# Seven block products in place of eight in the turned projections of a two-layer encoder step

## The chip, the cores and the metric

The kernel runs on one core of one Trainium2 chip. The metric is device microseconds of one execution, the median of the runs. Engines are named as the profile does: PE is TensorE (matrix products and transposes), DVE is VectorE, ACT is ScalarE, POOL is GpSimd, SP is SyncE, which issues most DMAs; each runs its own queue in order.

## What is computed

A step of an encoder with two layers, over 2048 prompt tokens and 64 new frames ("sample"), d = 1024, 16 heads of 64, in float32.

```python
q, k, v, gate = split(rms_norm(x, norm_a) @ w_in_a, 4)      # layer a, 1024 -> 4 x 1024
o = band_attend(q, k, v, rel_bias_a)                          # own chunk of 64 and 8 before it
x = x + (o * silu(gate)) @ w_out_a
k, v = split(rms_norm(x, norm_kv) @ w_kv, 2)                  # shared keys and values of layer b
q, gate = split(rms_norm(x, norm_b) @ w_in_b, 2)
o = stick_breaking_attend(q, [cache_b_k, k], [cache_b_v, v])
y = rms_norm(x + (o * silu(gate)) @ w_out_b, norm_f)
```

Outputs are y for prompt and sample, and the new keys and values of both layers. The inputs are drawn at random in float32, as are the weights.

## The kernel before

The program is one instruction stream per engine. Four stages follow one another: projections of layer a, its attention (with the output projection and the late jobs beside it), projections of layer b, its attention.

**Numbers in two parts.** A float32 operand of a product is held as h + l in the format fp32r: ScalarE copies x to h, VectorE makes l = x - h (`split`, line 211; with the norm's weight as a factor, `scaled_split`). A product of two such operands is three matmuls per block of 128 inputs, hh, hl and lh (`mm3`, line 229), 24 for 1024 inputs.

**Projections** (`projections`, line 240) run twice, for `L` "a" and "b". The tokens are two halves of 1024 (`HALF`); the 64 new frames stand behind the first half's columns. First come the *values*: for each of 17 tiles of 128 tokens x is loaded, normed (`normed`), transposed on TensorE (`turned`) and split (`parted`) into `x_own` (first half) or `x_big` (second half); with x as the stationary operand and 512 columns of value weights moving, 24 matmuls give 512 value columns of a tile. All 17 tiles pass for the first 512 columns, then again for the second. In layer a the values are split and stored; in layer b they are written out and into a scratch tensor `v_raw`.

Then come the *turned* projections, whose results stand with features on partitions and tokens along the row (keys, queries, gates). A job is one kind and one head pair (`hp`, 128 output columns), 24 jobs per layer. Its weights are loaded raw by ScalarE's DMA queue, scaled and split to `wh`, `wl`, and are stationary; x moves. The first half with the new frames takes chunks of 364, 362 and 362 columns, the second half two of 512 (`HALVES`). Each chunk has a PSUM bank of its own (`ps_t`, tag `mm`, five banks), which ScalarE and VectorE split (gates: SiLU) into a row buffer that is stored. Some jobs of the second half are not made here (`DEFER`): keys in a, gates and queries in b. They are the *late jobs* that run beside the attention (`late_job`, line 736; `lwh`, `lwl`, `ps_j`), in a with raw weights loaded again into `lraw` (buffer tag `og`), in b with split weights that the first stage stored (`KEPT`). Keys are also turned back into rows by TensorE for the output (`natural`, `ps_n`, `kn`).

**Staged work** is spread between the jobs by count (`stages`): caches are loaded, transposed or differenced, split and stored for the attention (`stage_cache`, `stage_bias`, `stage_diff`, `stage_w_out`). Layer b's attention uses differences of neighbouring value rows. For the cached rows, `stage_diff` ("cache") loads two shifted tiles and subtracts on GpSimd; for the new ones ("new", 34 steps) it does the same from `v_raw`, in layer b's turned stage.

**Order.** Inside the attention stages the order of every engine's instructions is written out by hand (`order`, `Beat`). In the projections the compiler's scheduler orders them by its own estimate of times, starting from the program's order. Buffers with the same tag share memory in a ring of `bufs`; a new tile waits for the last use of the one it replaces. `opool` holds the tags `oh`, `ol`, `og`, `xr`, `big` holds two tiles of 32 KB per partition that are x of the second half, later the output weights.

## Time and profile before

| what | us |
|---|---|
| median of 3 runs | 3265.88 (3264.77 to 3266.47) |
| the profiled execution, its time | 3270.1 |
| its span, first to last instruction | 3268.3 |
| values of a | 9.3 to 212.5 |
| turned projections of a | 212.5 to 678.7 |
| attention of a | 678.7 to 1418.6 |
| values of b | 1418.6 to 1621.2 |
| turned projections of b | 1621.2 to 2019.8 |
| attention of b | 2019.8 to 3268.3 |

How to read it: in a row of a group, the number behind x is the count, then come busy time in us, the mean ns of one instruction, and idle time of the engine before them with what ended it. A row of a window has its bounds and length, the busy time and count of PE, PEld (weight loads), DVE, ACT and POOL, the granted TensorE clock (1.00 is full speed), the share of the DMA engines and GB/s; a window asked for one tile counts that tile's instructions alone. A row of the timeline has start, duration, engine, line, operation, out<-in, shape and count. Matmuls are pipelined: a 512-column one shows some 0.39 us, while the next starts well before its end, so the cost of one in a stream is the distance between starts. Nearly all lines are L92, the helper through which the engines are called, so groups are told apart by their tiles.

### The profile page before, as it was taken

What the parts mean: (1) busy time and instruction counts of PE and PEld (TensorE: products, weight loads), DVE (VectorE), ACT (ScalarE), POOL (GpSimd) and SP (SyncE); (2) the same over time, 40 slices, a digit from 0 to 9 for tenths busy, and PEclk for the clock granted to TensorE, in tenths of its full rate; (3) what the DMA queues carried; (4) which work ended last, traced back from release to release, by engine and by line L of the source; (5) the groups of instructions that cost most, each with busy time, mean ns of one, the idle gap of its engine ahead of it and who ended that gap; (6) DMA issues with size and microseconds to landing.
All of it is one profiled execution on the core that took longest, in us unless ns stands there. A gap on an engine that the chain in (4) does not pass through costs nothing.

```text
span 3268.3 us, 53340 instructions
## 1 busy us (share of the span) xinstructions
PE 3199.2 (98%) x17928; PEld 2784.4 (85%) x17928; DVE 1872.0 (57%) x3786; ACT 1711.0 (52%) x3719; POOL 1291.8 (40%) x1950
## 2 busy tenths in 40 slices
PE   8999999999998999999999999999999999999999
PEld 7889999988887898878889999788888888888877
DVE  4225431157777776232043333788878888888873
ACT  5234322258887776143143442566666666666662
POOL 3001210035655554020044200344467777777761
PEclk9999999999999999999999999999999999999999
DMA  6359972387899993554399998977835566355523
GB/s 203 121 184 362 345 280 79 118 248 218 237 259 263 245 237 117 173 178 133 109 342 358 347 349 291 247 211 197 217 121 158 147 193 194 117 144 143 136 72 120
DMA packets 457209, 671.08 MB, mean 205 GB/s; under 512 B 48885, under 2 KB 258837, under 8 KB 456934
## 3 DMA queue, kind: packets, MB, share of 16 engines
q1 hardware_dynamic: 395174, 608.14, 60.9%
q10 hardware_dynamic: 61760, 59.52, 5.6%
q8 instruction: 143, 2.34, 0.3%
q14 instruction: 132, 1.08, 0.1%
HBM read 408.78 MB, written 258.76 MB: 204 GB/s over the span
## 4 chain that ended last, share of the span: by engine, by line
PE 76%; issue 7%; DVE 6%; DMA 6%; ACT 2%; POOL 2%; SPq 0%; POOLq 0%; ACTq 0%; DVEq 0%
PE ps_t L92 24%; PE ps_v L92 11%; PE acc L92 10%; PE z L92 9%; PE wt L92 9%; PE ps_j L92 6%; PE ps_o L92 5%; DVE s L92 2%; DVE pl L92 2%; DMA kt<-k_b 1%; PE ps_tr L92 1%; DMA q<-q_a 1%; DMA keys<-k_a 1%; DMA gate_b<-sg 1%; ACT ph L92 1%
## 5 line engine op out<-in xcount | busy, mean ns | idle before, releaser
L92 DVE TENSOR_TENSOR pl<-wt,ph 128x512 fp32r<-128x512 f32 (+1 forms) x864 | 552.0, 655 | 110.9 <-ACT ph L92 107.2
L92 ACT ACTIVATE ph<-wt 128x512 fp32r<-128x512 f32 (+1 forms) x864 | 485.2, 578 | 194.9 <-PE wt L92 180.7
L92 PE MATMUL ps_t<-x_own,wh 128*128 128x362 f32 (+1 forms) x2304 | 568.4, 327 | 0.0
L92 PE MATMUL wt<-ident,s 128*128 128x128 f32 x3472 | 552.2, 274 | 10.3 <-DVE pl L92 6.7
L92 PEld LDWEIGHTS wt<-ident,s 128*128 128x128 f32 x3472 | 418.2, 141 | 86.4 <-DVE pl L92 13.6
L92 ACT ACTIVATE f<-z 128x512 f32<-128x512 f32 (+4 forms) x680 | 355.0, 535 | 199.5 <-PE z L92 134.2
L92 PEld LDWEIGHTS ps_t<-x_own,wh 128*128 128x128 f32 x2304 | 405.0, 188 | 1.8
L92 POOL TENSOR_TENSOR s<-f,s 128x256 f32<-128x256 f32 x416 | 360.5, 868 | 102.5 <-DVE s L92 93.8
L92 PE MATMUL z<-kt,q 128*128 128x512 f32 (+3 forms) x1280 | 373.1, 379 | 9.8 <-DMA q<-q_b 5.3
L92 PE MATMUL acc<-ph,vt 128*128 128x512 f32 (+3 forms) x1088 | 374.5, 379 | 4.6 <-ACT ot L92 2.4
L92 PE MATMUL ps_t<-x_own,wl 128*128 128x362 f32 (+1 forms) x1152 | 376.6, 327 | 0.0
L92 PE MATMUL acc<-pl,vt 128*128 128x512 f32 (+3 forms) x1088 | 363.7, 367 | 9.2 <-DVE pl L92 9.0
L92 POOL TENSOR_SCALAR s<-s,rc 128x640 f32<-128x640 f32 (+5 forms) x264 | 201.5, 768 | 429.5 <-DMA q<-q_a 223.5
L92 PE MATMUL ps_o<-big,oh 128*128 128x512 f32 x1088 | 336.2, 392 | 0.0
L92 POOL TENSOR_TENSOR two<-f 128x256 f32<-128x256 f32 x416 | 259.4, 625 | 164.0 <-ACT f L92 149.3
L92 DVE TENSOR_TENSOR_SCAN s<-two,s,own 128x256 f32<-128x256 f32 x408 | 300.3, 739 | 36.7 <-POOL two L92 35.4
L92 PEld LDWEIGHTS z<-kt,q 128*128 128x128 f32 x1280 | 220.6, 190 | 40.7 <-ACT f L92 11.1
L92 PE MATMUL ps_j<-big,lwh 128*128 128x512 f32 x768 | 245.7, 396 | 1.2 <-DVE pl L92 0.6
L92 PE MATMUL ps_t<-big,wh 128*128 128x512 f32 x768 | 238.9, 391 | 0.0
L92 PEld LDWEIGHTS ps_o<-big,oh 128*128 128x128 f32 x1088 | 202.4, 188 | 41.0 <-DVE pl L92 0.2
L92 PEld LDWEIGHTS acc<-pl,vt 128*128 128x128 f32 x1088 | 194.3, 190 | 41.9 <-DVE pl L92 25.7
L92 DVE CUSTOM_DVE_ANT_0 s<-z,bias 128x640 f32<-128x640 f32 (+4 forms) x256 | 184.8, 733 | 73.9 <-PE wt L92 53.3
(148 smaller groups left out, 5510.3 us busy)
## 6 DMA issues: line engine op xcount, KB each, us to landing
vt<-v_b SPq DMA_DIRECT2D x80, 512.0 KB, 5.2
v_b<-vs SPq DMA_DIRECT2D x64, 512.0 KB, 6.4
q<-q_a SPq DMA_DIRECT2D x128, 256.0 KB, 5.9
q<-q_b SPq DMA_DIRECT2D x128, 256.0 KB, 4.3
vt<-v_a SPq DMA_DIRECT2D x48, 512.0 KB, 7.9
kt<-k_b SPq DMA_DIRECT2D x96, 256.0 KB, 5.7
keys<-k_a SPq DMA_DIRECT2D x80, 256.0 KB, 7.4
v_a<-vs ACTq DMA_DIRECT2D x32, 512.0 KB, 2.7
```

What stands on the lines that cost most here:

```text
L92: ins = op(*args, **kwargs)
```

## The change

It rearranges `projections` and what feeds it.

1. **Seven products for eight.** Two head pairs (256 output columns) and the two chunks of 512 tokens of one half, over two halves of the 1024 inputs, are a 2 x 2 by 2 x 2 block product. Strassen's scheme (in Winograd's form) makes it with seven block products. Each is 4 input blocks x 3 matmuls of 512 columns. Sums of x (`mix`: adds on GpSimd and VectorE, then splits) are made during the values, differences of weights (`weights_of`) per pair on GpSimd; results are put together in PSUM (bank `x` is added to three times, bank `z` twice) and on VectorE.
2. **One half at a time.** Values of the first half and the new frames, then 12 pairs; values of the second half, then 8 pairs (a) or 4 (b). The value weights are loaded and split in each half. Raw weights come for a pair, 2 x 512 KB; they are scaled on GpSimd before the split.
3. **The new frames** are no longer columns of a moving operand: `x_new` (h and l side by side) is stationary and 256 weight columns move, 16 matmuls per pair of the first half, then two transposes.
4. **Differences of the new values** are made with the values: a DMA inside SBUF shifts the tile by one row, one row goes through `v_raw`, VectorE subtracts, and the split result is stored from SyncE's queue. `stage_diff` keeps the cached rows only.
5. **Staged work** is spread anew: a's first half takes caches, biases and eight key caches, a's second half 16 differences of the cache, b's first half the other 16 and the other key caches, b's second half the output weights. `big1` becomes three tiles (`Pieces`). `x_own` loses the new frames' columns. Stored weights (b) have the pair's layout.

```diff
+            def mix(hf, u, tmp):
...
+                for x, k0, c in zip(tmp, (0, 0, 4, 4), (c1, c2, c2, c1)):
+                    h, l = xs[hf]
+                    for ks, part in rows_of(l, k0, slice(c, c + P)):
+                        whole = f32(h[:, k0 + ks.start : k0 + ks.stop, c : c + P])
+                        gps.tensor_tensor(x[:, ks], whole, f32(part), ALU.add)
+                a11, a21, a22, a12 = tmp
+                dve.tensor_tensor(a22, a21, a22, ALU.add)
+                split(*into(hf, 0, u), a22)
+                dve.tensor_tensor(a21, a11, a21, ALU.subtract)
+                if hf:
+                    split(*into(hf, 3, u), a21)
+                dve.tensor_tensor(a11, a22, a11, ALU.subtract)
+                split(*into(hf, 1, u), a11)
+                dve.tensor_tensor(a12, a12, a11, ALU.subtract)
+                split(*into(hf, 2, u), a12)
...
+                prev = vps[i % 2]
+                nc.sync.dma_start(prev[1:n], vn[: n - 1])
+                nc.sync.dma_start(vraw[r0 + n : r0 + n + 1, cols], vn[n - 1 : n])
...
+                else:
+                    nc.sync.dma_start(prev[0:1], vraw[r0 : r0 + 1, cols])
+                dve.tensor_tensor(prev[:n], prev[:n], vn, ALU.subtract)
+                store(prev[:n], nc.sync.dma_start)
...
+                def scale():
+                    for k in range(NK):
+                        r = raw[k // 4][:, k % 4]
+                        gps.tensor_scalar(r, r, g[:, k : k + 1], 1.0, ALU.mult, ALU.mult)
+
+                def whole(i):
+                    split(*forms[i], raw[i].rearrange("p k (b c) -> p b k c", b=2))
...
+                def less(i, out, x, y):
+                    gps.tensor_tensor(out, x, y, ALU.subtract)
+                    split(ts[i][:, 0], ts[i][:, 1], out)
+
+                return load, scale, [
+                    partial(whole, 0),
+                    partial(less, 0, r1[:, :, up], r1[:, :, up], r1[:, :, lo]),
+                    partial(whole, 1),
+                    partial(less, 1, r2[:, :, up], r2[:, :, up], r1[:, :, up]),
+                    partial(less, 3, r2[:, :, lo], r2[:, :, lo], r2[:, :, up]),
+                    partial(less, 2, r1[:, :, lo], r2[:, :, up], r1[:, :, lo]),
+                ]
+
+            def times(ps, x, w, begin):
+                for k in range(4):
+                    mm(ps, w[0](k), x[0](k), start=(begin and k == 0), stop=False, skip_group_check=True)
+                    mm(ps, w[0](k), x[1](k), start=False, stop=False, skip_group_check=True)
+                    mm(ps, w[1](k), x[0](k), start=False, stop=(k == 3), skip_group_check=True)
...
+                def plain(ps):
+                    c = pool.tile([P, CH], F32, name="c", tag="c", bufs=CS[L])
+                    act.activation(c, ps, AF.Copy)
+                    return c
+
+                def leave(b, t0, src):
+                    at = slice(r0 + t0 * CH, r0 + t0 * CH + CH)
+                    hl = pool.tile([P, 2, CH], F32R, name="hl", tag="hl", bufs=4)
...
+                    split(hl[:, 0], hl[:, 1], src)
+                    put(L, kind, hp + b, at, hl)
+                    row = hf * HALF + t0 * CH - first
+                    if kind == "k" and row >= 0:
+                        natural(pool, src, 0, P, 4, prompt[row : row + CH, (hp + b) * P : (hp + b) * P + P])
...
+                x = psum.tile([P, CH], F32, name="ps_x", tag="mm", bufs=5)
+                times(x, quarter(hf, 0, 0), w11, True)
+                c1 = plain(x)
+                between(0)
+                nn = new_frames() if hf == 0 else None
+                z = psum.tile([P, CH], F32, name="ps_z", tag="mm", bufs=5)
+                times(z, mixed(hf, 0), t1, True)
+                c5 = plain(z)
+                between(1)
+                times(x, mixed(hf, 1), t2, False)
+                u2 = plain(x)
+                if hf == 0:
+                    new_turned(nn)
+                between(2)
+                times(z, mixed(hf, 2), w22, False)
+                dve.tensor_tensor(u2, z, u2, ALU.add)
+                leave(1, 0, u2)
+                between(3)
+                times(x, mixed(hf, 3), t3, False)
+                dve.tensor_tensor(c5, x, c5, ALU.add)
+                leave(1, 1, c5)
+                between(4)
+                y = psum.tile([P, CH], F32, name="ps_y", tag="mm", bufs=5)
+                times(y, quarter(hf, 1, 0), w21, True)
+                dve.tensor_tensor(c1, y, c1, ALU.add)
+                leave(0, 0, c1)
+                between(5)
+                times(x, quarter(hf, 1, 1), t4, False)
...
+                    at = {1: 1, 2: 1, 5: 2, 6: 2}
+
+                    def between(p):
+                        if p == 0 and i + 2 < len(made):
+                            made[i + 2][0]()
+                        if p == 4 and i + 2 < len(made):
+                            made[i + 2][1]()
+                        for _ in range(at.get(p, 0)):
+                            if steps:
+                                steps.pop(0)()
+                        for _ in range(-(-len(mine) // (7 - p))):
+                            mine.pop(0)(staging["pool"])
...
+                t4 = opool.tile([P, 2, 4, P], F32R, name="t4", tag="og", bufs=1)
...
+                for i, t in enumerate(seq):
+                    if i + 2 < len(seq):
+                        parted(seq[i + 2], turned(seq[i + 2], xts(seq[i + 2])))
+                    if i >= 4 and i < 8:
+                        mix(0, i - 4, [tmp[0], tmp[4 + i - 4], tmp[1], tmp[2]])
+                    values(0, 0, i, t, vws, pool, vps)
```

`times` is one of the seven products; `quarter` and `mixed` give a block of x or a sum of blocks, `forms` the weights whole (`b1`, `b2`, made by `whole`) and their differences (`t1` to `t4`, made by `less`); `between` places the next pair's weight steps and the staged work behind product p. The last pair of the first half also loads, norms and turns the first two tiles of the second half and its value weights.

More of the change, by code (lines that the diff above doesn't have):

```diff
@@ L56 @@
 TOK = [(t * P, min(P, T - t * P)) for t in range((T + P - 1) // P)]
+VN = dict(a=2, b=4)
+XT = dict(a=4, b=3)
+CS = dict(a=5, b=4)
 HALF = NP // 2
@@ L158, in big_pair, with big_parts @@
     def big_pair():
-        return [big.tile([P, NK, D], F32R, name=f"big{i}", tag=f"big{i}") for i in range(2)]
+        return [big.tile([P, NK, D], F32R, name="big0", tag="big0"), Pieces(big_parts(F32R))]
+    def big_parts(dtype, some=(0, 1, 2)):
+        return [big.tile([P, (4, 2, 2)[i], D], dtype, name=f"bigl{i}", tag=f"bigl{i}") for i in some]
     ident = cpool.tile([P, P], F32, name="ident")
@@ L184, in encoder_step @@
             o=[dram.tile([HP, P, CH if g < GROUPS else NS], F32, name=f"o_{L}{g}") for g in range(GROUPS + 1)],
-            w={x: dram.tile([2, P, NK, P], F32R, name=f"w_{L}{x[0]}{x[1]}") for x in DEFER[L] if L in KEPT},
+            w={
+                x: dram.tile([2, 2, P, 2, 4, P], F32R, name=f"w_{L}{x[0]}{x[1]}")
+                for x in DEFER[L] if L in KEPT and x[1] % 2 == 0
+            },
         )
@@ L454, in stage_cache, with stage_diff @@
         )
-    def stage_diff(where, t, half, pool):
+    def stage_diff(t, half, pool):
         cols, heads = slice(half * CH, half * CH + CH), slice(half * 8, half * 8 + 8)
@@ L747, in load @@
                 for i, part in enumerate((st["wh"], st["wl"])):
-                    sp.dma_start(f32(part), f32(lay[L]["w"][kind, hp][i]))
+                    src = lay[L]["w"][kind, hp & ~1][i, :, :, hp & 1]
+                    sp.dma_start(
+                        f32(part).rearrange("p (h k) c -> p h (k c)", h=2), f32(src).rearrange("h p k c -> p h (k c)")
+                    )
         def cut(k0):
@@ L1058, in first_stage @@
         load_g("b", a["norm_b"][0])
-        none = pool.tile([P, CH], F32, name="vcur", tag="vr", bufs=2)
-        gps.memset(none, 0.0)
-        for c in range(0, D, CH):
-            nc.sync.dma_start(vraw[0:1, c : c + CH], none[0:1])
         stage_cache("a", 0, 0, pool)
@@ L1088, in encoder_step @@
         o["a_k_s"],
-        staged,
+        [staged, diffs[:16]],
     )
@@ L1265, in encoder_step @@
         o["b_k_s"],
-        staged_b,
+        [staged_b, outs_b],
     )
```

535 lines of the change are left out of this document (342 added, 193 removed).

## The prediction, made before the changed kernel was run

> **What bounds the kernel now.** I read the page's busy shares and slices, then the stages as windows, then single stretches of the timeline.
>
> ```profile
> span 3268.3 us, 53340 instructions
> PE 3199.2 (98%) x17928; PEld 2784.4 (85%) x17928; DVE 1872.0 (57%) x3786; ACT 1711.0 (52%) x3719; POOL 1291.8 (40%) x1950
> ```
> ```profile
> core 0: us, PE busy (x) PEld busy (x) DVE busy (x) ACT busy (x) POOL busy (x), PEclk, DMA share, GB/s
> 212.50:678.70 466.20, 465.13 (x2569) 433.92 (x2568) 144.91 (x390) 143.68 (x371) 45.80 (x43) 1.00 0.68 236
> 1418.60:1621.20 202.60, 202.06 (x928) 162.99 (x929) 38.03 (x73) 64.88 (x121) 28.57 (x34) 1.00 0.41 138
> 1621.20:2019.80 398.60, 398.18 (x2346) 379.76 (x2346) 152.78 (x321) 156.96 (x388) 90.57 (x74) 1.00 0.95 336
> ```
> The second and fourth rows are the turned projections of layers a and b. TensorE is busy for 465 of 466 us and 398 of 399; the other engines have over half of their time free. So here time is TensorE's queue, and each microsecond of matmul taken out counts, as long as nothing makes TensorE wait.
>
> **What is removed.** One job (8 input blocks, three products each) is 72 matmuls of 362 or 364 columns in the first half and 48 of 512 in the second. Two undisturbed jobs:
> ```profile
> 335.10:346.79 11.69, 11.69 (x73) 11.69 (x72) 1.75 (x3) 1.53 (x3) 1.00 0.94 327
> 346.79:357.69 10.90, 10.90 (x50) 9.02 (x49) 1.23 (x2) 1.07 (x2) 1.00 0.90 315
> ```
> So a pair of jobs takes 2 x 11.69 = 23.38 us in the first half, 21.80 in the second, and a 512-column matmul 10.90/48 = 0.227. A pair is now seven products of 12 matmuls: 84 x 0.227 = 19.07 us. In the first half come 16 matmuls of 256 columns for the new frames and two short transposes. No row has back-to-back matmuls of 256 columns in one stream; the neighbours are 128 and 320:
> ```profile
> 14.59 1.09 PE L92 MATMUL ps_tr<-ident,xt 128*128 128x128 f32 x8
> 15.44 0.48 PE L92 MATMUL ps_v<-vwl,x_own 128*128 128x512 f32 x1
> ...
> 688.27 1.33 PE L92 MATMUL z<-keys,q 128*128 128x320 f32 x8
> 689.44 0.62 PE L92 MATMUL ps_j<-big,lwh 128*128 128x512 f32 x2
> ```
> From start to next start: 0.85/8 = 0.106 and 1.17/8 = 0.146. I take 0.13, so 2.1 us (1.7 to 2.3), and 0.2 for the transposes. First half: 23.38 - 21.37 = 2.0 us a pair, 24 pairs, 48 us; the sixteen key jobs lose a sample transpose each, 16 x 0.11 = 2. Second half: 21.80 - 19.07 = 2.73, 12 pairs (8 in a, 4 in b; the rest stays in the attention), 33 us. **Gross gain 82 us** (77 to 92). Values, x transposes, cache transposes and attention keep their matmuls.
>
> **What is added beside it.** Durations:
> ```profile
> L92 POOL TENSOR_TENSOR vprev<-vprev,vcur 128x512 f32<-128x512 f32 x64 | 83.6, 1308 | 193.3 <-DMA vprev<-in_cache_b_v 133.8 <-DMA vprev<-v_raw 28.4 <-DMA vcur<-in_cache_b_v 12.3
> L92 POOL TENSOR_SCALAR s<-s,rc 128x256 f32<-128x256 f32 x16 | 7.8, 485 | 13.9 <-DVE rc L92 7.0 <-PE wt L92 4.1 <-PE z L92 2.6
> L92 ACT ACTIVATE junk<-xt 128x1024 bf16<-128x1024 f32 x32 | 33.8, 1057 | 63.6 <-DMA xt<-in_x_prompt 30.2 <-DMA xt<-x 29.7 <-issue 2.3
> L92 ACT ACTIVATE vn<-ps_v 128x512 f32<-128x512 f32 x40 | 23.7, 593 | 101.1 <-PE ps_v L92 95.9 <-DVE vs L92 4.5 <-DVE x_own L92 0.6
> L92 DVE TENSOR_TENSOR vs<-ps_v,vs 128x512 fp32r<-128x512 f32 x32 | 22.1, 691 | 99.1 <-ACT vs L92 99.1
> ```
> Per pair: GpSimd 8 scalings x 0.485 + 4 differences x 1.31 = 9.1 us. ScalarE two whole splits x 1.06, four of differences, three plain copies and four results at 0.6: 8.7, and 3.0 more for b's key rows. VectorE 4 x 0.69 + 2 x 1.38 for the splits, 3 x 0.69 sums, 4 x 0.69 results, 0.4 for the new frames: 10.8. Staged work adds 2 to 3 us to each. All of it fits into 19 to 21 us, beside TensorE; at nothing, while it comes on time.
>
> The new wait is on the accumulators. Before, each result had a bank of five to itself. Now bank x is added to again after ScalarE's copy, and only one other product, 12 x 0.227 = 2.72 us, lies between (z likewise). The copy takes 0.6, so it may start some 2 us late; then TensorE stops. Behind a late instruction on ScalarE stand all its copies. How late is ScalarE today?
> ```profile
> 1656.84 0.47 ACT L92 ACTIVATE both<-ps_t 128x362 fp32r<-128x362 f32 x1
> 1663.13 0.60 ACT L92 ACTIVATE kn<-ps_n 128x512 f32<-128x512 f32 x1 [5.82 <-DMA out_b_k_s<-kn]
> 1663.63 0.47 ACT L92 ACTIVATE both<-ps_t 128x362 fp32r<-128x362 f32 x1
> ```
> ```profile
> 1659.58 0.33 PE L92 MATMUL ps_t<-x_own,wl 128*128 128x362 f32 x1
> ```
> ```profile
> ACT vs L92 <- POOL vprev L92: 34.1, 14, 4.7
> ACT kn L92 <- DMA out_b_k_s<-kn: 9.7, 3, 5.8
> ACT kn L92 <- DMA out_b_k_p<-kn: 5.5, 6, 1.9
> ```
> The chunk finished at 1659.9 and was read at 1663.63, because a row copy ahead of it waited for a store; five banks hid that, one product wouldn't. Such waits (window 1630 to 2020) sum to 49 us of 390; over 36 pairs, 24 x 21.4 + 12 x 19.1 = 743 us, that is 94 at most, and nothing at least, as 2 us of each is covered. I take **30 us**: nearer to the lower third, since the new values' differences leave this stage.
>
> Handovers. Layer a's first attention job loads its raw weights into the buffer `og`, which the last pair now holds as `t4` until its last product:
> ```profile
> L92 DVE SCALAR_TENSOR_TENSOR lwl<-lraw,g_a,lwh x64: 326/353/1394, 655.3 to 936.4; 128x128 fp32r<-128x128 f32 x64
> DMA to landing us min/median/max: 4.5/4.9/11.0
> ```
> ```profile
> 678.51 0.39 PE L92 MATMUL ps_t<-big,wl 128*128 128x512 f32 x1
> 678.74 0.62 PE L92 MATMUL ps_j<-big,lwh 128*128 128x512 f32 x2
> ```
> Today the two stages touch. Load 4.9, its issue, and the first split's two halves at some 0.35: about 6 us idle (0 if other work is ready). A pause costs more than itself here:
> ```profile
> 1017.00:1027.00 10.00, 0.70 (x6) 0.47 (x5) 0.60 (x1) 2.83 (x6) 0.00 (x0) 0.78 0.88 232
> 1027.00:1030.00 3.00, 2.29 (x9) 1.89 (x9) 3.00 (x9) 1.47 (x3) 2.59 (x3) 0.50 1.04 257
> 1030.00:1032.00 2.00, 2.00 (x8) 1.51 (x7) 1.15 (x4) 1.64 (x4) 1.90 (x3) 0.50 1.08 254
> 1032.00:1035.00 3.00, 3.00 (x21) 3.00 (x20) 2.78 (x8) 2.38 (x6) 1.61 (x2) 0.85 1.10 271
> ```
> After that pause the clock stood at 0.50 for nearly 6 us, 3 us lost; I add half of it: 7.5. (The Trainium skill, "TensorE: Matmul & The Clock Gate", Part 1, halves the clock after an idle window of about 3.4 us and gives it back after as much work; the rows agree in kind, and by it my 6 us pause would cost up to 3 more.) Layer b's late weights need `ol`, held until product six of the last pair ends, 2.7 us before its end, and land after
> ```profile
> DMA to landing us min/median/max: 4.4/6.3/11.3
> ```
> 6.3 us: 4 us late (0 to 9). In the first values pass the sums of x add 4 x (7 x 0.69) = 19 us to VectorE over four tiles. A values matmul takes (202.6 - 136 x 0.106)/800 = 0.235 us, a tile 24 of them and 8 transposes, 6.5 us, in which VectorE has
> ```profile
> 40.00:60.00 20.00, 20.00 (x100) 16.47 (x100) 6.65 (x14) 8.74 (x17) 5.64 (x7) 1.00 0.58 159
> ```
> a third of the time taken: about 2 us behind, then eight weight splits, 3 us before pass two, twice: 6 (0 to 12). In the second half the pairs' buffers lie where the values' lay, and in b the last tile's copy, shift, difference and store end some 10 us after its matmul: 4 (0 to 12). **Handovers 21.5 us.**
>
> The new values' differences: 34 steps with two loads each leave the pair stage, and so do GpSimd's 34 x 1.31 us; beside the values stand one shift in SBUF, a row out and a row in, VectorE's difference and a store. SyncE then issues six transfers a tile, at
> ```profile
> 671.62 3.26 SPq L136 DMA_DIRECT2D keys<-k_a  x4
> ```
> up to 0.8 us each 4.9 of the second pass's 5.6 us. Its stores wait for VectorE, and loads of x queue behind; two tiles ahead, 11 us, cover that. Without the cover TensorE waits for x. I count nothing. Weights are loaded as 36 x 1 MB for 48 x 0.5 MB, and values' weights twice, beside a DMA share that was 0.95 already in b and loses 34 x 0.5 MB.
>
> Sum: -82 + 30 + 21.5 = -30.5. The profiled execution took 3270.1 us, its span 3268.3, the median 3265.88; against the median **3235 us**.
>
> **Rivals.** *Clean run*: the copies are ordered well, little waits: -82 + 10 = 3194. For it: 2 us of cover per join, engines half idle. Against: the late reads above. 0.18.
>
> *VectorE against GpSimd, slower*: the same weight split takes, over the whole run,
> ```profile
> L92 DVE SCALAR_TENSOR_TENSOR wl<-wraw,g_kv,wh x64: 339/351/1458, 1544.7 to 1775.8; 128x128 fp32r<-128x128 f32 x64
> ```
> 0.35 us, but up to 1.46 while GpSimd works: +1.1. Up to eleven of VectorE's instructions in a pair have both inputs in SBUF like this one, and GpSimd works 9 to 12 us of a pair. If each is held so, VectorE has 13 + 12 = 25 us against 19 to 21, and TensorE waits some 4.5 x 36 = 160: 3266 - 82 + 22 + 160 = 3366. It decides from (82 - 22)/36 = 1.7 us of TensorE's wait per pair on. Against: the median is 0.351, so most were not held. 0.20 for slower, most of it short of that full price. (The Trainium skill, "SBUF — State Buffer", "Who interferes with whom", says that a VectorE instruction with two SBUF inputs and a GpSimd one that reads SBUF exclude each other for a whole instruction; the maximum agrees, the median shows how seldom it hits today.)
>
> *Given back*: joins cost 55 to 60 us: 3259 to 3272, within 0.2%: 0.10. That it doesn't do what it says: 84 for 96 matmuls is in the text; none.
>
> **Numbers.** Forecast 3235 (3212 to 3259): 0.52. A measurement tells about 0.2%, 6.5 us, from no change: faster 0.70, same 0.10, slower 0.20. Range 3190 (gross 91, losses 15) to 3300, which leaves out the far end of the slower rival.
>
> **What will show it.** Right: matmuls of the pairs fall by about 1170 (4608 and 16 sample transposes before; 36 x 84 + 24 x 18 after), idle TensorE in the two pair stages totals 20 to 40 us, ended by ScalarE or VectorE; a gap of 5 to 9 us before a's first `ps_j`. Wrong: those gaps absent (clean), two-input VectorE rows well over 1 us on average (slower), or a 512-column matmul longer than 0.227.

## The result, and the profile after

The changed kernel takes **3599.61 us** (median of 4 runs, 3597.26 to 3601.53), the kernel before 3265.99 us: a ratio of 1.1022, 95% interval 1.1003 to 1.1041. It is 10% slower. The prediction was 3235 us with a range up to 3300, so it is wrong in sign and outside its range.

The page of the profile after, its span, busy shares and the slices of clock and transfers (each digit of a slice row is a tenth, 40 slices):
```profile
span 3595.5 us, 52143 instructions
...
PE 3190.8 (89%) x16760; PEld 2650.4 (74%) x16760; DVE 2247.6 (63%) x3944; ACT 1873.4 (52%) x3743; POOL 1695.6 (47%) x2377
```
```profile
PEclk9999999999999999775999876899999999999999
DMA  4776457588999845222988322797683548554423
```
The matmuls fell from 17928 to 16760, by 1168 where about 1170 were forecast, yet TensorE is busy for nearly as long as before (3191 us against 3199) in a span that is 327 us longer. The slices say where: in two places, at about 1440 to 1710 us and at 1980 to 2250, the clock falls to 0.5 to 0.8 and the transfers to 0.2 and 0.3. When TensorE, clock and transfers all go down together, a wait for one slow thing is the first guess.

The windows by stage (projections of layer a, its attention, projections of b, its attention) of before:
```profile
core 0: us, PE busy (x) PEld busy (x) DVE busy (x) ACT busy (x) POOL busy (x), PEclk, DMA share, GB/s
9.00:679.00 670.00, 667.98 (x3500) 598.41 (x3499) 204.73 (x497) 214.91 (x503) 74.08 (x77) 1.00 0.61 210
679.00:1419.00 740.00, 713.51 (x4306) 629.48 (x4304) 491.07 (x1291) 498.04 (x1133) 338.81 (x385) 0.99 0.80 220
1419.00:2020.00 601.00, 600.07 (x3273) 542.62 (x3272) 190.46 (x395) 221.58 (x510) 119.13 (x108) 1.00 0.77 269
2020.00:3268.00 1248.00, 1215.93 (x6848) 1012.29 (x6846) 983.64 (x1601) 772.40 (x1572) 758.50 (x1372) 1.00 0.58 163
```
and of the changed kernel:
```profile
9.00:668.00 659.00, 635.28 (x2888) 513.02 (x2888) 397.51 (x551) 295.60 (x506) 317.86 (x330) 0.99 0.59 203
668.00:1423.00 755.00, 719.38 (x4305) 634.23 (x4304) 494.02 (x1302) 500.70 (x1140) 339.01 (x386) 0.98 0.78 218
1423.00:2355.00 932.00, 620.28 (x2706) 490.86 (x2707) 371.34 (x489) 301.33 (x520) 279.09 (x281) 0.82 0.52 183
2355.00:3595.00 1240.00, 1213.84 (x6855) 1010.76 (x6854) 983.61 (x1600) 772.96 (x1575) 758.36 (x1372) 1.00 0.57 164
```
All of the loss lies in layer b's projections: 932 us for 601. TensorE stands still there for 932 - 620 = 312 us, and its 620 us of work are no less than before although 567 instructions are gone, because the clock averages 0.82. Only layer b makes differences of its new values. Its two largest waits, of all engines, are (the engine and the tile that waits, what it waits for; us in total, times, longest):
```profile
ACT vs L113 <- DVE vps L113: 353.5, 32, 16.1
DVE vps L113 <- DMA vps<-vn: 291.8, 28, 17.3
```
`vps` holds the shifted tile. VectorE waits for the transfer that fills it, ScalarE for VectorE. The chain of waits in a piece of the values stage (start, us, what) shows one such transfer at work:
```profile
1610.51 13.15 DMA vps<-vn
1623.69 0.70 DVE vps L113
...
1625.00 0.59 ACT vn L113
...
1627.17 13.44 DMA v_raw<-vn
...
1641.30 13.09 DMA vps<-vn
```
The shift `prev[1:n] <- vn[:n-1]` moves 127 rows, 254 KB, inside SBUF, and takes 13.1 us; the one row behind it in the same queue, 2 KB, lands only when the shift has. By the landing signals in the trace (the semaphore updates of the transfers) the 32 shifts of 127 rows took 12.8 to 19.5 us, 14.1 in the median; two more have 63 rows. In layer b's pair stage of before, sixteen DMA engines moved 336 GB/s at a busy share of 0.95, which is 22 GB/s for one engine, and 254 KB (260,096 bytes) at 22 GB/s is 11.8 us. So the shift looks like the work of one engine, and the packets of the trace show it: from 1619 to 1623 us a packet of 2 KB, one row, starts every 80 ns and takes 84 ns, and the mean busy share of the sixteen engines is 0.07, about one sixteenth:
```profile
1619.00:1623.00 4.00, 0.00 (x0) 0.00 (x0) 0.00 (x0) 0.00 (x0) 0.00 (x0) 0.50 0.07 26
```
The Trainium skill, "DMA: Bandwidth & Descriptors", section "Why a DMA increments its semaphore by 16 and not by 1", states the rule that fits: the number of engines is the largest one up to 16 that divides the row count, and 127 rows put everything on one. 127 is a prime. The kernel before has the remedy in its own text: the cached tile that is shifted in the same way goes in pieces of 112 and 15 rows.

### The profile page after: what moved, and what is told of

Its sections match the earlier page's. It is cut to its first block, busy times and chain, and to the rows that moved or that the text cites. A ratio compares the mean times of both kernels' runs of the same rounds, so it can differ in the third digit from the quotient of the medians.

```text
span 3595.5 us, 52143 instructions
## 1 busy us (share of the span) xinstructions
PE 3190.8 (89%) x16760; PEld 2650.4 (74%) x16760; DVE 2247.6 (63%) x3944; ACT 1873.4 (52%) x3743; POOL 1695.6 (47%) x2377
## 4 chain that ended last, share of the span: by engine, by line
PE 31%; DMA 11%; DVE 6%; issue 4%; ACT 2%; POOL 2%; SPq 2%; ACTq 0%; POOLq 0%; DVEq 0%
PE acc L113 6%; PE z L113 6%; PE wt L113 5%; DMA vps<-vn 5%; PE ps_j L113 5%; PE ps_x L113 3%; DMA v_raw<-vn 3%; PE ps_o L113 3%; DVE s L113 2%; DVE pl L113 2%; PE ps_z L113 2%; SPq L419 1%; PE ps_y L113 1%; POOL wraw L113 1%; DMA q<-q_b 1%
## 5 line engine op out<-in xcount | busy, mean ns | idle before, releaser
L113 PEld LDWEIGHTS wt<-ident,s 128*128 128x128 f32 x3472 | 417.1, 140 | 84.1 <-DVE pl L113 13.4
L113 PE MATMUL ps_x<-x_own,t 128*128 128x512 f32 x864 | 221.7, 405 | 68.1 <-DVE t L113 48.5
L113 PEld LDWEIGHTS ps_x<-x_own,t 128*128 128x128 f32 x864 | 163.2, 192 | 110.2 <-ACT c L113 62.8
L113 DVE TENSOR_TENSOR vps<-vps,vn 128x512 f32<-128x512 f32 (+1 forms) x34 | 23.5, 692 | 341.5 <-DMA vps<-vn 291.8
L113 DVE TENSOR_TENSOR_SCAN s<-f,own 128x128 f32<-128x128 f32 (+4 forms) x264 | 202.4, 788 | 29.6 <-ACT f L113 29.2
L113 PEld LDWEIGHTS acc<-ph,vt 128*128 128x128 f32 x1088 | 196.7, 190 | 26.2 <-ACT ph L113 5.4
L113 POOL TENSOR_TENSOR wraw<-wraw 128x512 f32<-128x512 f32 x96 | 146.5, 1539 | 146.9 <-DVE b2l L113 77.8
L113 PE MATMUL ps_o<-big,oh 128*128 128x512 f32 x544 | 213.9, 393 | 0.0
```

The costliest lines, as they stand in the source:

```text
L113: ins = op(*args, **kwargs)
```

## The experiments

Sixteen kernels were run, in five groups; the kernel before ran beside each group (medians 3263.8 to 3266.9 us). A ratio is to those runs.

| what ran | us | ratio and interval | projections a | attention a | projections b | attention b |
|---|---|---|---|---|---|---|
| before | 3265.99 | | 678.5 | 740.1 | 601.0 | 1248.7 |
| the change | 3599.61 | 1.1022 (1.1003 to 1.1041) | 667.8 | 755.2 | 932.3 | 1240.2 |
| 1 shift 112 + 15 | 3317.47 | 1.0169 (1.0152 to 1.0186) | 664.7 | 757.2 | 651.1 | 1238.9 |
| 2 shift 113 + 14 | 3553.12 | one run | 668.5 | 755.5 | 890.4 | 1236.7 |
| 3 no row in | 3575.32 | one run | 667.7 | 758.5 | 910.1 | 1237.2 |
| 4 no shift, no row in | 3292.24 | one run | 665.6 | 758.3 | 628.0 | 1238.6 |
| 5 products alone | 3369.91 | 1.0323 (1.0308 to 1.0338) | 704.6 | 756.7 | 626.7 | 1281.3 |
| 6 differences alone | 3599.56 | one run | 678.0 | 737.2 | 942.0 | 1240.6 |
| 7 the same, 112 + 15 | 3279.33 | 1.0049 (1.0032 to 1.0066) | 677.6 | 737.2 | 619.8 | 1239.9 |
| 8 run 1, own place for t4 | 3306.59 | 1.0123 (1.0106 to 1.0140) | 676.1 | 742.6 | 650.9 | 1236.8 |
| 9 run 8, row direct | 3301.44 | 1.0109 (1.0092 to 1.0126) | 674.7 | 738.4 | 644.7 | 1239.2 |
| 10 run 9, tails apart | 3292.25 | 1.0083 (1.0067 to 1.0098) | 676.6 | 745.2 | 632.0 | 1242.5 |
| 11 run 10, transfers alone | 3292.20 | one run | 674.8 | 743.8 | 632.2 | 1239.6 |
| 12 run 10 in order | 3295.88 | 1.0093 (1.0074 to 1.0112) | 672.8 | 750.1 | 626.6 | 1242.3 |
| 13 run 12 unstaged | 3336.75 | one run | 674.2 | 829.3 | 589.2 | 1241.9 |
| 14 run 7 unstaged | 3319.32 | one run | 679.0 | 790.5 | 605.8 | 1242.2 |
| 15 run 12, copies by VectorE | 3287.49 | one run | 673.4 | 741.7 | 630.9 | 1239.7 |
| 16 run 7, all cured | 3262.70 | 0.9997 (0.9988 to 1.0006) | 678.3 | 741.2 | 603.5 | 1241.3 |

The last four columns are of the one profiled execution of each: the projections end with the start of the last product of their pairs (layer a's begin with the span), the attention with the first values product of layer b or with the span. Profiles of stages that no edit touched differ by up to 12 us (attention a of runs 9 and 12), so smaller steps are not read from these columns.

### The shift

**Run 1**, the shift in two pieces:
```
-                nc.sync.dma_start(prev[1:n], vn[: n - 1])
+                for x, m in ((0, 112), (112, 15)) if n == P else ((0, 48), (48, 15)):
+                    nc.sync.dma_start(prev[x + 1 : x + 1 + m], vn[x : x + m])
```


> The shift of a tile by one row, 127 rows in one transfer, is split into 112 rows and 15. Theory A (127 rows of one transfer go through one of the sixteen DMA engines, since 127 has no other divisor, so 254 KB take some 13 us instead of 3): the shift lands in 3 to 4 us, the two values stages of layer b fall from 361 us together to 205 to 225, the median from 3600 to 3230 to 3290. Theory B (a transfer inside SBUF is slow whatever its rows): both parts together still take 13 us, 3580 to 3620. Theory C (the round trip of one row through memory is the long link): under 60 us gained, 3540 to 3600.

Measured: 3317.47 us, 282 us less. For one tile the chain of waits now has the piece of 15 rows and then that of 112:
```profile
1503.43 2.33 DMA vps<-vn
1507.07 4.58 DMA vps<-vn
```
So one line holds 282 of the 333.6 us lost. The level is 27 to 87 us above what was expected, and the time is still above that of before: something else costs too.

**Run 2**, two pieces again, of 113 (a prime) and 14 rows, to tell the count of rows from the count of transfers:
```
+                for x, m in ((0, 113), (113, 14)) if n == P else ...
```


> As the run with 112 and 15 rows, but split into 113 and 14; 113 is a prime number too. Theory A: the 113 rows still go through one engine, some 11.6 us of 13, the time falls by no more than 50 us from 3600: 3550 to 3610. Rival (two transfers at once are what helps, not their row counts): as with 112 and 15, 3230 to 3290.

Measured: 3553.12 us. SyncE issues both pieces of a tile (first row, its timeline), the 14 rows 0.7 us behind the 113, and the chain of waits has the second piece, which lands behind the first:
```profile
1508.82 1.52 SPq L419 DMA_DIRECT2D vps<-vn  x2
```
```profile
1509.52 11.44 DMA vps<-vn
```
By the landing signals the 113 rows of this tile took 12.0 us, from 1508.82 to 1520.78. Over the whole run a piece of 113 rows took 11.7 to 18.0 us, 13.1 in the median; in run 1 a piece of 112 took 2.6 to 6.7, 3.2 in the median. One row more makes that difference, and two pieces as such gain only 46 of the 334 us. The number of rows decides, as the rule says: the 113 rows, too, go out one packet every 80 ns.

**Run 3** keeps the shift of 127 rows and replaces the row that comes in from `v_raw` by zeros (the first row of each difference is left out); **run 4** has neither the shift nor the row in, and VectorE subtracts a tile from itself (the differences of the new values are left out). In both, the row still goes out to `v_raw`.

> The shift stays one transfer of 127 rows; the one row that each tile takes from the tile before it is not read back from memory but set to zero by GpSimd (this part of the differences is left out). Theory A: the shift alone sets the pace, 13 us land as before, 3480 to 3600. Theory C: the values stages of b fall to some 215 us together, 3240 to 3300.

> Shift and row are both left out: VectorE subtracts a tile from itself, the rest (split, store) stays; differences are not computed. Theory A and C: the floor of this stage, values of b 205 to 215 us together, 3220 to 3280, within 20 us of the run with 112 and 15 rows by theory A. Theory D (VectorE's work or the stores through SyncE's queue are too much for the stage): values stay above 300 us, over 3500.

Measured: 3575.32 and 3292.24 us. Without the row in, the long shift still costs nearly all, so the row's way back in isn't the long link. Without shift and row in, layer b's projections last 628 us, still 27 more than before; the time is 25 us under run 1 and 12 above what was expected, so there is a second cost that these transfers don't explain.

### The two halves of the change by themselves

**Run 5** is the seven products with the new values' differences staged beside the pairs, as before (`v_raw` written by ScalarE's queue; the cache's last sixteen differences back in layer a's first half). **Run 6** is the kernel before with the values' differences alone; **run 7** the same with the shift in pieces.

> The seven products and the half-by-half order stay; the new values' differences go back to where they were (v_raw rows stored by ScalarE's queue, subtracted by staged work of the pair stages), and the cache's last sixteen differences return to layer a's stage. So this is the change without its last clause. Theory A (the last clause costs: the shift, and also the tail of late splits on ScalarE before each pair stage of layer b): the tails go, the first pairs of layer b start within 5 us of idle TensorE, values of layer b back to about 206 us in sum, and the time is 3235 to 3265 us, at or under the kernel before. Theory B (the products' own joins and buffer handovers eat their gain, whoever makes the differences): pairs of layer b stay near 428 us in sum and the time is 3285 to 3320 us.

> The kernel before with only the last clause of the change: new values' differences made beside the values of layer b, tiles in order of rows, the shift as one transfer of 127 rows; projections by the plain three products. Theory A (one shift is about 13 us on one DMA engine, 34 of them in a stage that was 202 us, i.e. 6 us a tile): values of layer b last 400 to 480 us, time 3450 to 3560 us, clock of the span near 0.95. Theory B (the long shift hurts only beside the products' extra transfers and joins): values under 260 us, time under 3320 us.

> As the run with the last clause alone, but with the shift in pieces of 112 and 15 rows (48 and 15 for the sample). Theory A (only the one-engine transfer is dear): staged differences leave the pairs of layer b, values gain 10 to 20 us of ScalarE and VectorE work that TensorE mostly covers: 3255 to 3280 us. Theory C (making the differences with the values is dear by itself, through late splits in ScalarE's order): values of layer b over 225 us, first pair late by 10 us or more, 3285 to 3300 us.

Run 6, with plain projections, loses as much as the whole change: 3599.56 us. In its projections of layer b the windows are, for values, the gap behind them, and jobs:
```profile
1415.00:1872.00 457.00, 241.22 (x928) 188.49 (x928) 73.67 (x121) 75.70 (x139) 28.68 (x35) 0.75 0.24 87
1872.00:1957.00 85.00, 0.00 (x0) 0.00 (x0) 8.88 (x13) 6.37 (x11) 0.00 (x0) 0.53 0.20 72
1957.00:2357.00 400.00, 399.23 (x2343) 380.78 (x2344) 127.81 (x298) 141.81 (x360) 44.51 (x40) 0.99 0.73 252
```
The 34 shifts are issued between 1432.0 and 1947.0 us, one in 15.6 us, where a tile's products took 6 us before: the values stage has become a queue of shifts, 457 us for 202, and its last ones end 85 us after the last product. The time is 40 us above theory A's range, which did not count this gap. Run 7 has the values back at 202 us, but one gap is left between values and jobs:
```profile
1617.00:1634.00 17.00, 0.64 (x4) 0.21 (x2) 4.14 (x7) 3.00 (x7) 0.00 (x0) 0.65 0.48 157
```
```profile
PE ps_t L92 <- ACT wh L92: 16.4, 1, 16.4
```
which is about the 15 us by which it is slower. Here both expectations were half right: the time is where A had it, the late first job is C's. The chain of waits shows why it is late: the last split, which still reads `vps` in `og`, ends at 1627.9 us, and only then is the first raw weight loaded into the same place, in 5.4 us.

Run 5 missed both expectations: at 3370 us it is worse than B's. Part of that is my own arrangement of the staged work. In layer a's first half, where I had put sixteen differences more, TensorE waits for key blocks, and in the short second half of b 24 staged steps didn't end with their four pairs:
```profile
PE ps_c L113 <- DMA kr<-in_cache_b_k: 21.6, 3, 11.9
```
```profile
2091.62 7.45 DMA vprev<-v_raw
...
2099.09 10.88 DMA vt<-v_b
```
(the second one is the chain of waits after the last product of b's pairs; attention b is 33 us longer for it). So this run is an upper bound for the products alone, and it shows something else: with a half of the tokens at a time and fewer matmuls there is less room to hide staged work in.

### Handovers and the order of the queues

Runs 8 to 10 and 12 start from run 1 and mend one thing after the other. In **run 8** layer a's `t4` lies in the pool of its pair stage, not in `og`:
```
-            t4 = opool.tile([P, 2, 4, P], F32R, name="t4", tag="og", bufs=1)
+            home, tag = (own_forms, "t4") if L == "a" else (opool, "og")
+            t4 = home.tile([P, 2, 4, P], F32R, name="t4", tag=tag, bufs=1)
```


> The changed kernel with the shift in pieces (3317 us) and with the fourth mixed weight of layer a's second half in a place of its own, so that the first late weight block can be loaded during the last pairs. Theory A (the late start of the first late job, 15 us after the last product where it was 0.2 us before, is the shared place): the first late job starts within 5 us and the time is 3303 to 3310 us. Theory B (the start is set by SyncE's order or by something else): no change, 3313 to 3320 us.

Measured: 3306.59 us, 11 less. Products of the late jobs now stand among those of the last pair, from 665.1 us on, and the last product of a's pairs is followed at once by one of them (timeline):
```profile
676.13 0.39 PE L113 MATMUL ps_x<-big,t 128*128 128x512 f32 x1
676.36 0.39 PE L113 MATMUL ps_j<-big,lwh 128*128 128x512 f32 x1
```
The time is where theory A had it. In run 1 the first `ps_j` came 15.4 us after the last product, and TensorE was idle for 9.8 of them. The place `og` was the cause. (In part because late products now run within it, the column of projections a is 11 us longer than in run 1, and that of attention a 15 shorter.)

**Run 9** sends the last row of a tile straight to the next tile's place, in place of out to `v_raw` and back:
```
-                else:
-                    nc.sync.dma_start(prev[0:1], vraw[r0 : r0 + 1, cols])
+                if n == P and t % NK < NK - 1:
+                    nc.sync.dma_start(vps[(i + 1) % 2][0:1], vn[n - 1 : n])
```


> As the run with the fourth mixed weight in a place of its own (shift in pieces, 3307 us), and the last row of a value tile goes straight into the first row of the next tile's place instead of out to v_raw and back. Theory A (in SyncE's order the row's load waits for the row's store to land, and the next shift stands behind it: 5 to 6.5 us a tile at the end of the values): the last four differences follow each other within 3 us, the first pair of layer b's second half loses 8 to 12 us of its 21 idle, time 3285 to 3297 us. Theory B (the tail is the shift's own landing and the ScalarE and VectorE steps behind it): 3300 to 3309 us.

Measured: 3301.44 us; the intervals of 8 and 9 overlap, so the gain is a few us at most. The first pair of b's second half waits 19.0 us for `c` where it waited 21.0: theory B. What stands ahead of that copy is to be seen in run 1: first TensorE's largest wait in layer b's projections, then ScalarE's timeline, where the first product of the pair was done at about 1960 us:
```profile
PE ps_x L113 <- ACT c L113: 28.7, 2, 21.0
```
```profile
1971.27 0.63 ACT L113 ACTIVATE vs<-vps 128x512 fp32r<-128x512 f32 x1 [3.30 <-DVE vps L113]
...
1973.53 1.30 ACT L113 ACTIVATE vs<-vcur 128x512 fp32r<-128x512 f32 x2 [1.14 <-DMA vcur<-in_w_out_b]
1978.36 0.63 ACT L113 ACTIVATE vs<-vps 128x512 fp32r<-128x512 f32 x1 [3.52 <-DVE vps L113]
...
1982.87 1.21 ACT L113 ACTIVATE vs<-vcur 128x512 fp32r<-128x512 f32 x2 [2.44 <-DMA vcur<-in_w_out_b]
1984.74 0.63 ACT L113 ACTIVATE t<-wraw 128x512 fp32r<-128x512 f32 x1 [0.66 <-DMA v_b<-vs]
...
1985.83 0.60 ACT L113 ACTIVATE c<-ps_x 128x512 f32<-128x512 f32 x1
```
The bracket is the idle time before the instruction and what ended it. ScalarE does its work in order: splits of the last differences (each late by a shift), output weights that come from a transfer, mixed weights whose memory the last store still holds, and behind them all `c`, for which TensorE has been waiting for 21 us.

**Run 10** takes these apart: value copies and splits in a pool that outlives the values and that staged work reuses, `t4` of the first pair made later, no staged work in a first pair. In it that `t4` was made after a later raw block had been fetched into its source, so its first pairs multiply by a wrong `t4`; **run 12** has it before.
```
+            vpool = beside.enter_context(tc.tile_pool(name=f"tail1_{L}", bufs=1))
-                    values(1, 1, i, t, vws, pool, vps)
+                    values(1, 1, i, t, vws, vpool, vps)
-                    n = -(-len(staging["todo"]) // left) if left > 0 else 0
+                    n = -(-len(staging["todo"]) // left) if left > 0 and i else 0
```


> As the run before it, and: value copies and split differences lie in a pool of their own that outlives the values (the staged work reuses it), so that the pairs' tiles no longer lie on memory that the last differences still hold; the fourth mixed weight of the first pair is made after its first product; no staged work in the first pair. Theory A (what stands ahead of the first c copy on ScalarE is the wait for that memory and the staged splits): first pairs of layer b within 3 us of a quiet pair (22 and 19 us), time 3240 to 3265 us. Theory B (the pairs of layer b are held by the transfers, busy share 0.93 of sixteen engines in the first half's pairs, and not by the order): first pairs improve, but the sum of the first half's pairs stays over 295 us and the time is 3270 to 3290 us.

> As the earlier run with the tails apart, but the fourth mixed weight of the first pair is made after the first product and before the next raw block is fetched into its source. Theory A (that weight waited for a later block's transfer): the first pairs of the second halves lose 3 to 6 us each, time 3278 to 3288 us. Theory B (no matter): 3290 to 3297 us.

Measured: 3292.25 and 3295.88 us, the same within their runs (3291 to 3298, 3288 to 3299): the order of `t4` doesn't matter for the time. For run 10 theory B is the nearer: its first-half pairs last 304.4 us, the time is 2 us above its range; that the transfers are the reason is not shown by this. Run 12 is where its theory B had it. The first pairs improved (b's projections lost 18 us from run 9 to run 12), but b's first-half pairs still last 300.7 us in run 12.

### What the pairs of layer b have lost

In run 12 these pairs run at a transfer share of 0.89, and nearly every pair has staged work on ScalarE and VectorE. **Run 11** has the staged work of b as transfers alone (keys, cache differences, output weights: loaded and stored, not computed). **Run 13** leaves this work out of layer b (zeros are stored in its places during layer a's attention). **Run 14** does the same to run 7, the plain projections (there it is the keys and output weights).

> As the run before it, but layer b's staged work (the keys of its cache from the ninth block on, the cache's differences from the ninth tile on, the output weights) is done as transfers of the same bytes alone: loaded, and the loaded tile stored in place of high and low parts; the transposes, splits and subtractions are left out. Theory A (the staged ScalarE, VectorE and TensorE steps in the in-order queues hold the pairs): the pairs of layer b's first half fall to 262 to 275 us (TensorE loses 96 transposes, 10 us). Theory B (the transfers hold them): they fall by no more than the 10 us of transposes.

> As the run before it, with layer b's staged work left out: 24 key blocks of its cache, 16 cache differences, 16 blocks of output weights; their places are filled with zeros during layer a's attention instead. Theory A (this work, no longer covered by matmuls, holds the pairs through the in-order queues and the transfers): pairs of layer b's first half fall from about 304 to 262 to 272 us (10 of it the left-out transposes), of the second from 106 to 80 to 92 us, the time by 45 to 60 us. Theory B (the joins of the products by themselves): they fall by little more than the transposes, the time by under 20 us.

> The plain projections with the values' differences made with the values (shift in pieces, 3279 us), and the same kind of staged work left out of layer b (24 key blocks, 16 blocks of output weights; zeros during layer a's attention). Theory A (plain matmuls cover it): the pairs of layer b fall from 401 us by the 10 us of transposes, to 388 to 392 us. Theory B (it costs there too): under 385 us. Pair stages of layer b then compare as products against plain projections without staged work on either side.

Run 11: the first-half pairs fall from 304.4 to 273.4 us, as A had it, but the time doesn't, since a chain of key blocks, one place for load and store, ran on for 42 us before the second values. This kernel had made that chain itself, so the run says nothing more of the whole. In the first 100 us of the pairs, though, it tells the staged steps from the transfers (first row run 10, second row run 11):
```profile
1540.00:1640.00 100.00, 89.18 (x433) 71.66 (x432) 65.15 (x73) 49.14 (x87) 63.80 (x63) 0.98 0.96 330
1540.00:1640.00 100.00, 96.15 (x472) 78.79 (x471) 51.62 (x67) 45.98 (x80) 48.65 (x56) 0.98 1.02 357
```
Run 11 moves more there, 357 GB/s for 330, and TensorE waits less. So in this stretch it is the staged steps in the engines' queues, and not the transfers' share, that hold the pairs.

Runs 13 and 14 took longer in all (3337 and 3319 us), against the expectation: with the zeros stored in it, layer a's attention is 79 and 53 us longer than in runs 12 and 7. The comparison is in layer b alone. The windows of the pairs in run 12, and of values, pairs, values and pairs in run 13:
```profile
1541.00:1842.00 301.00, 288.38 (x1398) 234.78 (x1397) 171.66 (x213) 147.86 (x256) 141.88 (x153) 0.98 0.89 315
...
1946.00:2050.00 104.00, 87.92 (x396) 69.65 (x395) 62.63 (x76) 52.21 (x91) 41.42 (x39) 0.97 0.90 313
```
```profile
1503.00:1621.00 118.00, 109.76 (x481) 85.86 (x480) 85.10 (x110) 57.19 (x101) 52.17 (x45) 0.97 0.57 195
1621.00:1893.00 272.00, 268.29 (x1290) 220.05 (x1289) 135.16 (x171) 125.39 (x212) 119.50 (x137) 0.99 0.63 221
1893.00:1996.00 103.00, 99.52 (x450) 80.58 (x449) 65.00 (x97) 46.56 (x80) 49.83 (x45) 0.98 0.53 186
1996.00:2093.00 97.00, 87.19 (x398) 69.99 (x397) 49.66 (x58) 42.84 (x73) 39.08 (x39) 0.96 0.61 207
```
The pairs' 272 and 97 us are at the upper end of theory A's range in the first half and above it in the second; run 14's jobs take 387 us, between its two theories. The staged work costs the products 626.6 - 589.2 = 37 us of layer b, of which 10 are its 96 transposes; it costs the plain projections 619.8 - 605.8 = 14, which is little more than the transposes. So plain matmuls cover it and the products don't: 23 to 27 us. This is weaker than it looks: it rests on one profile of each kernel, and run 13 leaves out 16 cache differences that run 14 doesn't have in this layer. And with none of it, layer b's projections take 589 us with products and 606 - 16 = 590 without, leaving the gap of run 7 aside. Even unburdened, the products gain nothing that these columns can tell in this layer: the gain in the pairs goes into the slower values (118 + 103 us for 202) and the first pair of each half.

**Run 15** makes the copies `c` on VectorE:
```
-                    act.activation(c, ps, AF.Copy)
+                    dve.tensor_copy(c, ps)
```


> As the first run of these, with the copies of the accumulators that the products share (c) made by VectorE in place of ScalarE. Theory A (ScalarE's in-order queue, with staged copies and key rows ahead, is what makes the joins late): the waits for ScalarE's c go, part comes back as waits for VectorE, time 5 to 20 us less. Theory B (what is late is late on both, or VectorE is the busier): same or up to 30 us more.

Measured: 3287.49 us in one run, just under the fastest of run 12's runs (3288.43): less by 8 us, as A had it, but not clear of the spread. In the pairs of b's first half, TensorE's waits for ScalarE's `c` (6.3 and 4.3 us in two groups) turn into waits for VectorE's (4.9, 3.8 and 1.6), and b's projections are no shorter (630.9). So the joins are not ScalarE's fault alone: what is late is late on either.

### The differences, cured

**Run 16** is run 7 with the row sent directly, and the two places of `vps` in `xr`, which plain projections leave free, in place of `og`, into which the first weight block of the pairs is loaded:
```
-                    vps = opool.tile([P, 2, CH], F32, name="vps", tag="og", bufs=1)
+                    vps = opool.tile([P, 2, CH], F32, name="vps", tag="xr", bufs=2)
```


> Plain projections, values' differences made with the values: shift in pieces of 112 and 15 rows, last row straight to the next tile's place, and the differences' two places in xr, which plain projections leave free, instead of og, into which the first weight block of layer b's pair stage is loaded. Theory A (the 17 us gap between values and pairs was og): the gap is under 5 us and the time 3253 to 3266 us. Theory B (the gap was the late splits on ScalarE and the memory of the value tiles): gap over 10 us, time 3272 to 3282 us.

Measured: 3262.70 us, ratio 0.9997 (0.9988 to 1.0006). The gap is gone; over layer b's projections TensorE is busy for 599.0 of
```profile
1420.00:2023.00 603.00, 599.00 (x3271) 541.27 (x3270) 210.84 (x432) 222.81 (x509) 75.20 (x75) 1.00 0.70 242
```
603 us. This is where theory A had it. Cured of its three faults, the last clause of the change costs nothing and gains nothing that can be told. No run here beats the kernel before by more than the measurement tells.

## Why the prediction was wrong, point by point

**What bounds the kernel.** Right for the kernel before: TensorE's queue. In the changed kernel the values of layer b are bound by the shifts, which stand in a queue; TensorE idles there, and its clock falls. In run 1, where that is cured, TensorE is busy for 587 of the 651 us of layer b's projections, and VectorE, the next, for 388.

**Gross gain 82 us.** Right where nothing is late, at the lower end of the 77 to 92 that it gave. Four undisturbed first-half pairs of run 13, and one of the second half of run 12:
```profile
1787.20:1874.10 86.90, 86.90 (x410) 71.07 (x408) 52.14 (x58) 40.28 (x67) 38.51 (x40) 1.00 0.65 236
```
```profile
632.20:650.90 18.70, 18.70 (x82) 15.22 (x81) 7.89 (x9) 9.82 (x21) 6.35 (x5) 1.00 0.19 71
```
21.7 us a pair for the 21.37 forecast and 18.7 for 19.07: 24 x (23.38 - 21.7) + 12 x (21.80 - 18.7) = 77 us. The matmul count was right to within two.

**The new values' differences: "I count nothing".** This is the step that failed. It weighed the six issues on SyncE, and gave the shift in SBUF no duration of its own. A shift of 127 rows took 14.1 us in the median, 32 times, in a stage with 6 us a tile: 282 us (runs 1, 2 and 6). The cover of "two tiles ahead, 11 us" that the prediction named is less than one such transfer, which took 12.8 us at least. It also named the price of losing the cover ("TensorE waits for x"), and gave that no chance.

**Joins 30 and handovers 21.5 us.** Right in kind, undersized, and by enough that the forecast would have failed without the shift, too: run 1 takes 3317 us, and the range ended at 3300. Run 1, in which the shift is cured, has
```profile
9.00:665.00 656.00, 635.06 (x2889) 511.97 (x2888) 396.16 (x550) 294.36 (x504) 323.77 (x330) 0.99 0.60 204
665.00:1422.00 757.00, 718.22 (x4306) 632.98 (x4306) 494.43 (x1302) 501.23 (x1140) 339.91 (x386) 0.98 0.79 218
1422.00:2073.00 651.00, 586.85 (x2707) 470.58 (x2708) 387.62 (x489) 301.94 (x520) 287.86 (x281) 0.96 0.75 262
```
and so 21 + 64 = 85 us of idle TensorE in the projections, 82 more than before; 46 us less of its work where 77 were to be had; and 17 us more in attention a. The other 31 us of work are about what the mean clocks of 0.99 and 0.96 make of 635 and 587 us, by estimate 6 and 23. 82 + 31 + 17 = 130 us against the 51.5 forecast; 77 gained and some 10 in attention b leave 43, which is what the span shows (3311.9 against 3268.3). (Attention b is 6 to 12 us shorter in every run but run 5; run 5 alone has the new values' differences in the pairs, as before. In run 16 a wait of 5.3 us for `q` near its start is gone; the rest stays open.) In run 12, with tails and `og` mended too, the busy times are 640.65 and 582.55 us:
```profile
9.00:673.00 664.00, 640.65 (x2913) 515.33 (x2913) 395.35 (x565) 297.27 (x519) 315.21 (x330) 0.99 0.59 204
1423.00:2050.00 627.00, 582.55 (x2708) 468.23 (x2708) 383.31 (x489) 300.13 (x521) 284.57 (x281) 0.98 0.78 272
```
with 23 + 44 = 67 us idle: 45 us of work less, 65 of idle time more. By their parts:

- *The joins, 30 us.* In the pairs of both layers TensorE is idle for 66 us in run 1, 17 in a and 49 in b, the tails below among them, and for 45 in run 12.
- *`og` held as `t4`, 7.5 us.* Right: TensorE was idle for 9.8 us, and 11 us came back in the median of run 8.
- *The sums of x beside the values, 6 us (0 to 12).* TensorE is idle for 19 us in the values of run 1, 4 in a and 15 in b; in b the differences are made there too, and the shares are not told apart.
- *Layer b's late weights in `ol`, 4 us (0 to 9).* Not seen: in run 12 the first `ps_j` of this layer starts 1.5 us after the last product, with 0.7 us idle between.
- *The tail of the last differences before the pairs, 4 us (0 to 12), in b.* Mis-sized: one wait of 21 us in b's second half, and a like one of 7.7 in its first half, which the prediction hadn't counted. `vps` in `og` belongs here too: with plain projections the first job waited 16 us for it (run 7) and didn't in run 16, which also sends the row directly; the two shares are not told apart.
- *Staged work "fits into 19 to 21 us, beside TensorE; at nothing, while it comes on time".* It didn't: some 23 to 27 us in layer b (runs 12 to 14, one profile of each).
- *The transfers*, with a share of "0.95 already in b", were named and not priced. In the first 100 us of run 11's pairs more bytes moved and TensorE waited less, so there the in-order queues cost the time; for the whole 23 to 27 us it is not settled, as the rest of run 11 is spoiled by its own chain.

**The rivals.** The clean run is excluded: no run with the products comes near 3194 us. VectorE against GpSimd, which was to decide the slower side, is there at a fraction of the price. Run 1's VectorE rows (mean ns after the busy time), one with both inputs in SBUF and one with a bank of PSUM:
```profile
L113 DVE TENSOR_TENSOR hl<-c,hl 128x512 fp32r<-128x512 f32 x80 | 76.4, 977 | 20.1 <-ACT hl L113 18.4 <-DMA k_a<-nhl 0.7 <-DMA wraw<-in_w_in_a 0.7
L113 DVE TENSOR_TENSOR xr<-ps_o,xr 128x512 f32<-128x512 f32 x64 | 44.0, 687 | 114.0 <-PE ps_o L113 99.2 <-issue 12.6 <-POOL xr L113 1.7
```
0.98 us against 0.69: 0.3 us for each of eleven in a pair, not 1.1. That is 3 us a pair for an engine with time to spare; what it adds to the lateness of the joins wasn't measured by itself. The rule cited there from the Trainium skill ("SBUF — State Buffer", "Who interferes with whom") agrees in sign; the mean shows that it hits a part of them only.

**What was to show it.** The idle time in the two pair stages was to be 20 to 40 us. It was 175 us, 19 of them in layer a; its largest waits, 48.5 and 35.9 us, were ended by VectorE and ScalarE, as forecast, but the chain of waits behind them goes through the shifts. The fall of the matmuls came as forecast. Before a's first `ps_j` the gap was to be 5 to 9 us and was 15. A sign for a late shift wasn't on the list.

## What to carry to other kernels

Price every transfer that a change adds by its shape, not by its bytes: a shift by one row is 127 rows, which took 14.1 us in the median, and its 112 rows in a piece of their own 3.2. A stage that loses matmuls also loses cover: list what is staged beside it, in each in-order queue, before counting the saved matmuls as saved time. And a buffer lent to a new tile at the end of a stage is a wait at the start of the next; look up who loads into it first.

## What the hardware showed that was not expected

- Transfers inside SBUF of 127 rows of 2 KB took 12.8 to 19.5 us, those of 113 rows 11.7 to 18.0, those of 112 rows 2.6 to 6.7 (medians 14.1, 13.1 and 3.2 us).
- A row of 2 KB issued behind the long shift landed 13.4 us after its issue; the row's way back in was no long link (run 3).
- The stage with the pauses lost twice: in layer b's projections after the change TensorE was idle for 312 us, and the rest of its work, 17% fewer instructions, took 620 us for 600 at a mean clock of 0.82.
